# Triangular inverses of the RWKV-7 recurrence kept in a PSUM bank, with the factor stored by rows

## The chip, the cores and the metric

One core of a Trainium2 chip runs the whole kernel. The metric is device microseconds of one execution, as the median of several runs. The engines are named as in the profile: PE (matrix multiplies, with PEld for its weight loads), DVE (vector engine), ACT (scalar engine), POOL, and SP, whose queue issues the DMAs.

## The reference, cut to what matters

The kernel computes two decoder layers on 1024 tokens of width 1024. In each layer a normalised input goes through one input projection; its columns feed three token mixers (an RWKV-7 recurrence with 4 heads of 64, a dilated attention, a latent attention); an output projection and a SwiGLU feed-forward follow. The change lies in the recurrence, which the reference writes as a scan over tokens:

```python
def step(state, inp):
    r_t, w_t, k_t, v_t, kk_t, b_t = inp
    sa = jnp.einsum('bhvk,bhk->bhv', state, kk_t)
    state = (state * w_t[:, :, None, :] - sa[..., None] * b_t[:, :, None, :]
             + v_t[..., None] * k_t[:, :, None, :])
    y = jnp.einsum('bhvk,bhk->bhv', state, r_t)
    return state, y
```

The kernel does this in chunks of 64 tokens. Inside a chunk the terms `sa` depend on each other through a lower triangular 64x64 matrix, so each pair of chunk and head needs the inverse of a unit triangular matrix.

## The kernel before, in words

**Work and its order.** The 1024 tokens are two halves (`hf` 0 and 1) of 512; tiles are 128 partitions x 512 floats (a page in SBUF, a bank in PSUM). All steps are Python generators ("strands"). While the program is built, the class `Flow` plays them against a clock per engine: each helper books a cost (`tt` on DVE 1.04 ns a column and 65 ns, `vtrans` 1.1 ns a column and 65 ns, `acopy` 0.833 ns a column and 80 ns), a result is usable 150 ns (PE 230 ns) later (`LATENCY`, line 106), and the strand that can start first goes next (`run`, line 172), with a lower number as the stronger priority at ties. The order found so is the order of each engine's queue in the program, and an engine never leaves that order on the chip: if an instruction at the head of a queue waits, all behind it wait. The costs are guesses of the plan; the chip's are in the profile.

**Pages and banks.** `page`/`pages` take SBUF pages from a pool of 79, `bank` (line 351) takes one of the 8 PSUM banks, `free` gives them back. `in_proj` (line 1094), the input projection, runs with a weak priority (6) and asks with `bank("inp", 4)` (line 1142): it takes a bank only when at least 4 others stay free. One output tile of it is 24 matmuls; it is emptied by DVE in the first half of layer 0, otherwise by ACT (`evac`, line 1022). Its weights are fetched by `loader` (line 475): a DMA brings `wr`, ACT makes the rounded part `wh` and POOL (sometimes DVE) the rest `wl`; up to 6 such pairs lie ready (`ring`).

**The recurrence.** `recurrence(hf)` (line 1211) has priority 0 and runs four times in all (two layers, two halves). After the Gram matrices `Gm` (32 pairs of chunk and head, each 128 x 128, in `a1`) are there, it inverts the 32 triangular matrices, each as two 32x32 blocks on the diagonal that are then joined:

- Four DVE transposes (line 1425) write `NL`, 128 partitions x 32 x 32: partitions 0 to 63 hold the two diagonal blocks of all 32 pairs, and partitions 64 to 127 the same again. A partition's element is `NL[p, t, s]`, the factor of row t and column s.
- A DMA brings `first`, the rows of unit matrices, into the page `W` (line 1429); the lower and the upper 64 partitions hold the even and the odd rows.
- 31 steps of two DVE instructions each (lines 1432 to 1438). Step s works on n x m columns, n = s // 2 + 1 and m = 31 - s, 2856 columns over the 31 steps: the first instruction multiplies one column of `W` with one column of the factor into `tmp`, the second takes `tmp` from `W`. Each needs the result of the one before.
- Two ACT copies bring the halves of `W` together as `W2` (line 1442), two DVE transposes put the inverses into `TT` (line 1450), and one more makes `T1` in the tile `T1Y` (line 1454).
- `merge` (line 1457) joins the blocks: 32 small matmuls "mg" a half with `T1`, an ACT copy into `T1Y`, 32 more matmuls, an ACT copy into `TT`. Then the chunks follow one after the other.

Beside this run the input projection of the same or the next half and, in the first half, `rates` (line 1226), whose matmuls "lo" need `xw` from DVE.

Of the kernel before, what the change touches and what calls it, by code (L numbers as in the profile page):

```python
# [14 lines left out]
ALU = mybir.AluOpType  # L15
# [207 lines left out]
def cols(ap):  # L223
    n = 1
    for d in ap.shape[1:]:
        n *= d
    return n
# [3 lines left out]
def trunk(ctx: ExitStack, tc: tile.TileContext, xT, pos, vec, con, first, w_in, small, uq, uqr, ukv,  # L231
# [3 lines left out]
    F = Flow()  # L235
# [56 lines left out]
    def acopy(out, in_):  # L292
        F.op("act", cols(in_) * 0.833 + 80)
        nc.scalar.copy(out=out, in_=in_)  # L294
# [3 lines left out]
    def tt(eng, out, a, b, op):  # L298
        F.op(eng, cols(out) * (1.04 if eng == "dve" else 2.2) + 65)
        ENG[eng].tensor_tensor(out=out, in0=a, in1=b, op=op)  # L300
# [18 lines left out]
    def vtrans(out, in_):  # L319
        F.op("dve", cols(in_) * 1.1 + 65)  # L320
        nc.vector.transpose(out=out, in_=in_)

    def dma(out, in_, nbytes):

        s = F.cur
        start = max(s.at(), F.clock["dma"])
        F.clock["dma"] = start + max(450.0, nbytes / 360.0)
        nc.sync.dma_start(out=out, in_=in_)
        return F.clock["dma"] + 2000
# [21 lines left out]
    def bank(name="ps", keep=0, n=None):  # L351
        yield Need([banks], n or 1, keep)
        out = []
        for _ in range(n or 1):
            t = psp.tile([128, HALF], F32, tag="ps", name=name)
            owner[id(t)] = (banks, t, None)
            out.append(t)
        return out if n else out[0]
# [7 lines left out]
    def pages(where, names, dt=F32, keep=0, of=None):  # L366

        def taken(n):
            if of in reserve:
                reserve[of] -= n  # L370

        got = yield Need(lambda: [P[w] for w in where], len(names), keep, taken if of else None)
        of = of if of in reserve else None
        out = []
        for n, s in zip(names, got):
            n, d = n if isinstance(n, tuple) else (n, dt)
            t = s.pool.tile([128, HALF], d, tag="hp", name=n)
            owner[id(t)] = (s, t, of)
            out.append(t)
        return out  # L380

    def page(where, name, dt=F32, keep=0, of=None):
        return (yield from pages(where, [name], dt, keep, of))[0]

    def free(*tiles):
        for t in tiles:
            s, _, of = owner.pop(id(t))
            if of is few:
                F.give(few)
            elif of in reserve:  # L390
                reserve[of] += 1
            F.give(s)
# [213 lines left out]
    W = Lookup()  # L606
# [62 lines left out]
    def head_rsqrt(sq, col, guard, op):  # L669

        s = yield from bank("hsum")
        yield "pe"
        for c in range(4):
            mm(s[:, 2 * c:2 * c + 2], sq[:, c * 128:(c + 1) * 128], cons[:, CON[col]:CON[col] + 2], True, True)
        y = yield from rsqrt(s[:, 0:8], 8, guard, op)
        yield "dve"
        vcopy(sq.rearrange("p (a b) -> p a b", b=64), y.unsqueeze(2).to_broadcast([128, 8, 64]))
        yield "pe"
        for c in range(4):
            cs_ = slice(c * 128, (c + 1) * 128)  # L680
            transpose(s[:, cs_], sq[:, cs_])
        return s
# [33 lines left out]
    def events(*shape):  # L716
        if len(shape) == 1:
            return [Event() for _ in range(shape[0])]
        return [events(*shape[1:]) for _ in range(shape[0])]
# [247 lines left out]
    def layer(l):  # L967
# [243 lines left out]
        def recurrence(hf):  # L1211
# [4 lines left out]
            AP_ = ["gp"]  # L1216
# [83 lines left out]
            for j in range(2):  # L1300
# [4 lines left out]
                p = yield from head_rsqrt(sq, "hones", 1e-24, ALU.max)  # L1305
# [62 lines left out]
                p = yield from bank("bn")  # L1368
# [48 lines left out]


            NL = a1.tile([128, 32, 32], F32, tag="NL", name="NL")
            for hb in range(2):  # L1420
                src = Gm[32 * hb:32 * hb + 32, :, 32 * hb:32 * hb + 32].rearrange("p u t -> p t u")
                for ig in range(2):
                    o = 64 * ig + 32 * hb
                    yield "dve"
                    vtrans(NL[o:o + 32], src)
            w_init = Event()
            W_, tmp = yield from pages(AP_, ["W", "tmp"])
            yield "dma"
            F.set(w_init, None, dma(W_, first, 262144))
            yield w_init  # L1430
            Wt = W_.rearrange("p (i t) -> p i t", t=32)
            for s in range(31):
                n, m = s // 2 + 1, 31 - s
                t3 = tmp[:, 0:n * m].rearrange("p (i t) -> p i t", t=m)
                yield "dve"
                tt("dve", t3, Wt[:, 0:n, s:s + 1].to_broadcast([128, n, m]),
                   NL[:, s + 1:, s].unsqueeze(1).to_broadcast([128, n, m]), ALU.mult)
                tt("dve", Wt[:, 0:n, s + 1:], Wt[:, 0:n, s + 1:], t3, ALU.subtract)
            W2 = a1.tile([128, 16, 2, 32], F32, tag="NL", name="W2")
            for ig in range(2):  # L1440
                yield "act"
                acopy(W2[0:64, :, ig, :], Wt[64 * ig:64 * ig + 64])
            free(W_, tmp)
            yield "pool"
            F.op("pool", 1000)
            nc.gpsimd.memset(TT[32:64, :, 0:32], 0.0)
            for hb in range(2):
                r = slice(32 * hb, 32 * hb + 32)
                yield "dve"
                vtrans(TT[r, :, r].rearrange("p u t -> p t u"), W2[r].rearrange("p i g t -> p t (i g)"))  # L1450
            T1Y = a1.tile([128, 32, 32], F32, tag="NL", name="T1Y")
            T1, Ys = T1Y[0:32], T1Y
# [996 lines left out]
        for hf in range(2):  # L2449
            F.spawn(recurrence(hf), 0)  # L2450
# [179 lines left out]
```

## Time and profile before

| | |
|---|---|
| median of 3 runs | 2693.75 us (2692.81 to 2708.47) |
| the profiled execution | 2702.44 us, of which 2700.4 us lie between its first and last instruction (the span) |
| busy in the span | PE 2569.5 us, DVE 1865.0, POOL 1266.2, ACT 1146.0 |
| the four inverses, from the first transpose to `T1Y` | 126.8 to 177.9, 268.5 to 322.1, 1448.9 to 1491.4, 1615.9 to 1660.5 us |

Times in the rows are microseconds from the start of the span unless marked ns. In a timeline, the bracket behind an instruction gives the time for which its engine was idle before it, and what ended that. The tile `W2` shows under the name W, since it is read from W, and PEclk is the clock granted to PE as a share of the full one. Matmuls overlap, so the time that each shows is longer than the distance to the next.

### The profile page before, as it was taken

The page shows a single profiled execution, that of the slowest core. Times are in us where ns is not written, and L with a number is a line of the kernel's source. Part 1 is how long each engine was busy: PE and PEld are TensorE (multiplying, and loading weights), DVE is VectorE, ACT ScalarE, POOL GpSimd, SP SyncE. Part 2 cuts the span into 40 slices and gives each one's busy share as a digit, 9 for nine tenths or more (in the row PEclk, how much of TensorE's full clock was granted, in tenths as well). Part 3 has the DMA queues.
Part 4 walks back from the last instruction along what each step waited for, and adds up shares of the span by engine and source line. Part 5 has one row for each costly group of instructions (what it writes and reads, how often), then busy time and mean ns, then how long its engine had stood idle before and what let it go on. Part 6 is the DMA issues. An engine that isn't in the chain of part 4 may idle for free. (4 is left out here: it accounts for less than half of the span.)

```text
span 2700.4 us, 38578 instructions
## 1 busy us (share of the span) xinstructions
PE 2569.5 (95%) x13112; PEld 2055.7 (76%) x13112; DVE 1865.0 (69%) x3539; ACT 1146.0 (42%) x2312; POOL 1266.2 (47%) x978
## 2 busy tenths in 40 slices
PE   7989898999999999999999998999998999999998
PEld 6766765788777888888878676657887888888887
DVE  7988758765778676556578477577558876665556
ACT  5344357564434343322343433656644343333221
POOL 4635332346654444465554354223566444444561
PEclk9889899999999999999999898999999999999999
DMA  5222202026435444796332121101363454349861
GB/s 183 80 90 87 75 9 73 21 69 205 148 133 187 152 172 151 259 343 224 131 124 84 60 75 40 52 26 40 102 215 110 164 195 144 137 158 336 285 208 63
DMA packets 204772, 365.08 MB, mean 135 GB/s; under 512 B 23712, under 2 KB 38304, under 8 KB 204448
## 3 DMA queue, kind: packets, MB, share of 16 engines
q1 hardware_dynamic: 204576, 362.63, 39.3%
q8 instruction: 103, 1.69, 0.2%
q14 instruction: 93, 0.76, 0.1%
HBM read 253.22 MB, written 105.64 MB: 133 GB/s over the span
## 5 line engine op out<-in xcount | busy, mean ns | idle before, releaser
L300 POOL TENSOR_TENSOR wl<-wr,wh 128x512 fp32r<-128x512 f32 (+1 forms) x376 | 546.9, 1466 | 515.3 <-ACT wh L294 450.3
L265 PE MATMUL gu<-hhi,wh 128*128 128x512 f32 x1232 | 484.0, 393 | 18.5 <-ACT u L294 12.4
L265 PE MATMUL gu<-hhi,wl 128*128 128x512 f32 x1232 | 480.5, 391 | 1.1 <-POOL wl L300 1.0
L265 PE MATMUL gu<-hlo,wh 128*128 128x512 f32 x1232 | 481.4, 391 | 0.0
L294 ACT CAST wh<-wr 128x512 fp32r<-128x512 f32 (+1 forms) x496 | 287.3, 597 | 127.4 <-POOL wl L300 38.9
L265 PEld LDWEIGHTS gu<-hhi,wh 128*128 128x128 f32 x1232 | 232.5, 189 | 76.8 <-ACT u L294 15.3
L265 PEld LDWEIGHTS gu<-hhi,wl 128*128 128x128 f32 x1232 | 232.4, 189 | 50.9 <-POOL wl L300 2.0
L265 PEld LDWEIGHTS gu<-hlo,wh 128*128 128x128 f32 x1232 | 232.7, 189 | 47.2
L300 POOL TENSOR_TENSOR wl<-s,wh 128x512 fp32r<-128x512 f32 (+1 forms) x136 | 180.0, 1332 | 188.1 <-ACT wh L294 93.6
L265 PE MATMUL dn<-bhi,wh 128*128 128x512 f32 (+1 forms) x664 | 251.7, 380 | 0.7 <-issue 0.7
L265 PE MATMUL dn<-bhi,wl 128*128 128x512 f32 (+1 forms) x664 | 251.5, 379 | 0.0
L265 PE MATMUL dn<-blo,wh 128*128 128x512 f32 (+1 forms) x664 | 251.5, 379 | 0.0
L265 PE MATMUL inp<-hhi,wh 128*128 128x512 f32 x512 | 220.1, 430 | 14.5 <-ACT wh L294 14.5
L294 ACT CAST wh<-s 128x512 fp32r<-128x512 f32 (+1 forms) x204 | 116.6, 581 | 228.4 <-DVE s L300 198.2
L265 PE MATMUL inp<-hlo,wh 128*128 128x512 f32 x512 | 210.3, 411 | 0.0
L265 PE MATMUL inp<-hhi,wl 128*128 128x512 f32 x512 | 209.7, 410 | 0.5 <-POOL wl L300 0.3
L300 DVE TENSOR_TENSOR x<-x,dn 128x512 f32<-128x512 f32 (+1 forms) x160 | 104.5, 657 | 109.3 <-PE dn L265 82.2
L300 DVE TENSOR_TENSOR v<-u,gu 128x512 f32<-128x512 f32 x132 | 90.1, 682 | 128.6 <-PE gu L265 125.1
L300 POOL TENSOR_TENSOR v<-v 128x512 f32<-128x512 f32 x66 | 97.1, 1473 | 136.1 <-DVE v L300 127.0
L265 PEld LDWEIGHTS dn<-bhi,wh 128*128 128x128 f32 x664 | 124.9, 188 | 25.0 <-issue 1.5
L265 PEld LDWEIGHTS dn<-bhi,wl 128*128 128x128 f32 x664 | 124.9, 188 | 23.5
L265 PEld LDWEIGHTS dn<-blo,wh 128*128 128x128 f32 x664 | 124.9, 188 | 23.3
(314 smaller groups left out, 5536.0 us busy)
## 6 DMA issues: line engine op xcount, KB each, us to landing
wr<-in_w_in_dram SPq DMA_DIRECT2D x144, 256.0 KB
act_dram<-ahi SPq DMA_DIRECT2D x142, 256.0 KB
act_dram<-alo SPq DMA_DIRECT2D x142, 256.0 KB
bhi<-act_dram SPq DMA_DIRECT2D x142, 256.0 KB
blo<-act_dram SPq DMA_DIRECT2D x142, 256.0 KB
wr<-in_w_gate_dram SPq DMA_DIRECT2D x104, 256.0 KB
wr<-in_w_up_dram SPq DMA_DIRECT2D x104, 256.0 KB
wr<-in_w_down_dram SPq DMA_DIRECT2D x96, 192.0 KB
```

The costliest lines, as they stand in the source:

```text
L265: nc.tensor.matmul(out=out, lhsT=lhsT, rhs=rhs, start=start, stop=stop, **kw)
L294: nc.scalar.copy(out=out, in_=in_)
L300: ENG[eng].tensor_tensor(out=out, in0=a, in1=b, op=op)
```

## The change

The 64x512 halves stay as they are, but `W` becomes `Wp`, a PSUM bank. The DMA brings `first` into the page `tmp`, and a small strand `init` of priority 0 lets ACT copy it to the bank. Two DVE transposes rather than four write `NL`, only its partitions 0 to 63, and with the two axes exchanged, so that `NL[p, s, t]` has one step's factors side by side; one ACT copy repeats them in partitions 64 to 127. The steps read `NL[:, s, s+1:]`. The bank is given back where the page `W` was.

```diff
             NL = a1.tile([128, 32, 32], F32, tag="NL", name="NL")
+            tmp = yield from page(AP_, "tmp")
+            Wp = yield from bank("Wp")
+            yield "dma"
+            w_init, w_set = events(2)
+            F.set(w_init, None, dma(tmp, first, 262144))
+
+            def init():
+                yield w_init
+                yield "act"
+                acopy(Wp, tmp)
+                F.set(w_set)
+
+            F.spawn(init(), 0)
             for hb in range(2):
                 src = Gm[32 * hb:32 * hb + 32, :, 32 * hb:32 * hb + 32].rearrange("p u t -> p t u")
-                for ig in range(2):
-                    o = 64 * ig + 32 * hb
-                    yield "dve"
-                    vtrans(NL[o:o + 32], src)
-            w_init = Event()
-            W_, tmp = yield from pages(AP_, ["W", "tmp"])
-            yield "dma"
-            F.set(w_init, None, dma(W_, first, 262144))
-            yield w_init
-            Wt = W_.rearrange("p (i t) -> p i t", t=32)
+                o = 32 * hb
+                yield "dve"
+                vtrans(NL[o:o + 32].rearrange("p s t -> p t s"), src)
+            yield "act"
+            acopy(NL[64:128], NL[0:64])
+            yield w_set
+            Wt = Wp.rearrange("p (i t) -> p i t", t=32)
             for s in range(31):
                 n, m = s // 2 + 1, 31 - s
                 t3 = tmp[:, 0:n * m].rearrange("p (i t) -> p i t", t=m)
                 yield "dve"
                 tt("dve", t3, Wt[:, 0:n, s:s + 1].to_broadcast([128, n, m]),
-                   NL[:, s + 1:, s].unsqueeze(1).to_broadcast([128, n, m]), ALU.mult)
+                   NL[:, s, s + 1:].unsqueeze(1).to_broadcast([128, n, m]), ALU.mult)
                 tt("dve", Wt[:, 0:n, s + 1:], Wt[:, 0:n, s + 1:], t3, ALU.subtract)
             W2 = a1.tile([128, 16, 2, 32], F32, tag="NL", name="W2")
             for ig in range(2):
                 yield "act"
                 acopy(W2[0:64, :, ig, :], Wt[64 * ig:64 * ig + 64])
-            free(W_, tmp)
+            free(Wp, tmp)
```

## Rows read from the trace of the kernel before

**Rows 1.** The page, busy tenths of PE and its granted clock in 40 slices.
```profile
PE   7989898999999999999999998999998999999998
...
PEclk9889899999999999999999898999999999999999
```

**Rows 2.** Windows over the four inverses: busy time of each engine.
```profile
126.80:177.90 51.10, 39.18 (x196) 32.74 (x194) 48.86 (x93) 15.25 (x24) 19.19 (x14) 0.91 0.45 144
268.50:322.10 53.60, 44.25 (x230) 38.05 (x230) 49.36 (x111) 15.98 (x29) 20.28 (x17) 0.91 0.25 87
...
sum 191.80, PE 158.44 PEld 135.60 DVE 178.72 ACT 54.75 POOL 75.55; mean PE 39.61 PEld 33.90 DVE 44.68 ACT 13.69 POOL 18.89
```

**Rows 3.** Timeline of PE: its long waits at the end of the inverses.
```profile
176.64 0.79 PE L265 MATMUL lo<-xw,whi 128*128 128x512 f32 x1 [11.92 <-DVE xw L300]
...
322.13 3.62 PE L265 MATMUL mg<-T1Y,Gm 32*32 32x32 f32 x64 [7.68 <-DVE T1Y L321]
...
1491.34 3.62 PE L265 MATMUL mg<-T1Y,Gm 32*32 32x32 f32 x64 [7.21 <-DVE T1Y L321]
...
1653.87 0.80 PE L265 MATMUL inp<-hhi,wh 128*128 128x512 f32 x1 [4.75 <-ACT wh L294]
...
1672.48 3.62 PE L265 MATMUL mg<-TT,T1Y 32*32 32x32 f32 x64 [5.99 <-ACT T1Y L294]
```

**Rows 4.** Windows behind these waits; the third number from the right is PEclk.
```profile
176.60:186.30 9.70, 9.66 (x24) 6.45 (x25) 6.63 (x19) 4.37 (x6) 2.41 (x2) 0.51 0.11 43
322.10:333.60 11.50, 11.47 (x148) 10.38 (x149) 2.54 (x4) 4.56 (x9) 2.57 (x3) 0.50 0.13 36
1491.30:1504.20 12.90, 12.86 (x150) 11.00 (x150) 1.51 (x3) 4.87 (x10) 2.86 (x3) 0.52 0.35 120
1653.80:1657.10 3.30, 3.10 (x7) 2.00 (x8) 2.75 (x3) 3.25 (x8) 3.20 (x3) 0.51 0.09 16
1672.40:1684.60 12.20, 12.12 (x92) 9.57 (x93) 5.79 (x7) 4.27 (x10) 2.17 (x2) 0.50 0.03 6
```

**Rows 5.** Timeline of ACT: what stands behind its copies of W in its queue.
```profile
1484.33 1.25 ACT L294 COPY W<-W 64x512 f32<-64x512 f32 x2 [13.65 <-DVE W L300]
1485.48 0.57 ACT L294 COPY pj<-inp 128x512 f32<-128x512 f32 x1
...
1652.41 0.62 ACT L294 COPY W<-W 64x512 f32<-64x512 f32 x1 [14.10 <-DVE W L300]
...
1653.20 0.62 ACT L294 CAST wh<-wr 128x512 fp32r<-128x512 f32 x1
```

**Rows 6.** Windows of the steps' instructions alone (tile tmp), one inverse and the sum.
```profile
1448.90:1491.40 42.50, 25.00 (x62) 0.94 0.34 110
...
sum 191.80, DVE 98.76; mean DVE 24.69
```

**Rows 7.** Groups of DVE instructions by shape: busy us, mean ns, idle before.
```profile
L300 DVE TENSOR_TENSOR W<-W,tmp 128x30 f32<-128x30 f32 x8 | 1.5, 189 | 0.2
L300 DVE TENSOR_TENSOR W<-W,tmp 128x130 f32<-128x130 f32 x4 | 1.2, 296 | 0.1
L300 DVE TENSOR_TENSOR W<-W,tmp 128x128 f32<-128x128 f32 x4 | 1.2, 293 | 0.1
L300 DVE TENSOR_TENSOR tmp<-W,NL 128x16 f32<-128x16 f32 x4 | 0.7, 180 | 0.1
L300 DVE TENSOR_TENSOR tmp<-W,NL 128x128 f32<-128x128 f32 x4 | 1.6, 400 | 0.1
L300 DVE TENSOR_TENSOR pl<-tp,ph 128x128 fp32r<-128x128 f32 x16 | 4.6, 286 | 2.0 <-ACT ph L294 1.9
L321 DVE STREAM_TRANSPOSE NL<-Gm 32x1024 f32<-32x1024 f32 x16 | 32.2, 2010 | 0.3
L321 DVE STREAM_TRANSPOSE TT<-W 32x1024 f32<-32x1024 f32 x8 | 17.8, 2228 | 3.3 <-ACT W L294 3.2
```

**Rows 8.** Tile Gm on DVE: duration ns min/median/max (operand G in PSUM).
```profile
L300 DVE TENSOR_TENSOR Gm<-G,tabs x32: 672/680/692, 89.6 to 1615.3; 128x512 f32<-128x512 f32 x32
```

**Rows 9.** Timeline of DVE inside the third inverse: two steps' instructions.
```profile
1465.47 1.34 DVE L300 TENSOR_TENSOR tmp<-W,NL 128x110 f32<-128x110 f32 x1
1466.85 0.27 DVE L300 TENSOR_TENSOR W<-W,tmp 128x110 f32<-128x110 f32 x1
```

**Rows 10.** Timeline of POOL at the same time.
```profile
1461.26 5.33 POOL L300 TENSOR_TENSOR wl<-wr,wh 128x512 fp32r<-128x512 f32 x4 [9.49 <-PE vB L265]
```

**Rows 11.** Groups of ACT copies: busy us, mean ns, idle before.
```profile
L294 ACT COPY W<-W 64x512 f32<-64x512 f32 x8 | 4.9, 617 | 41.0 <-DVE W L300 41.0
L294 ACT COPY tabs<-sq 128x1 f32<-128x1 f32 x1 | 0.2, 186 | 0.0
```

**Rows 12.** Window of 15 us in which PE runs the projection at full clock.
```profile
135.00:150.00 15.00, 15.00 (x68) 12.43 (x67) 14.00 (x34) 1.91 (x4) 5.09 (x4) 1.00 0.26 76
```

## The prediction

> **What bounds the kernel now.** I read the page's 40 slices first. PE is busy nine tenths or more in nearly all of them, so a microsecond on another engine counts only where PE waits for it. Among the few slices with an eight for PE are those of the inverses, and the granted clock falls there too [rows 1]. The windows over the four inverses come next: DVE is busy 178.72 of 191.8 us there and PE only 158.44 [rows 2]. So in these stretches DVE is the bound, and PE runs beside it on the input projection until the plan's order brings an instruction that needs the inverse. The timeline of PE shows those points: 11.92, 7.68, 7.21, 4.75 and 5.99 us, 37.6 us in sum [rows 3]. Two wait for `T1Y`, the end of the inverse itself. The first waits for `xw`, which stands on DVE behind the inverse's last transposes. The fourth waits for a weight `wh`, whose cast stands on ACT behind the copy of W, and ACT had then waited 14.10 us for the last step [rows 5]. The fifth waits for ACT's copy into `T1Y`, which stood behind attention casts that waited for DVE. All five are one thing: DVE comes to the end of the 31 steps later than the plan thought.
>
> Each wait has a sequel. Behind it PE runs at 0.50 to 0.52 of its clock, the lower level of 1.2 GHz, for 9.7, 11.5, 12.9, 3.3 and 12.2 us, 49.6 us in all, and is busy all the time [rows 4]. At full clock that work would take about half.
>
> **The transposes of NL.** Four at 2.01 us go [rows 7], 8.04 us. Two come that read as before and write with a stride; the nearest row is TT<-W, strided on both sides, 2.23 us [rows 7], so 4.46 us. The ACT copy of 64x1024 is new: 186 ns for one column and 617 for 512 [rows 11] give 0.84 ns a column and 1.05 us, and I add 0.3 us for the two handovers. The path gets 8.04 - 5.8 = 2.2 us shorter, DVE is relieved of 3.6. Bounds for the two transposes: 2.01 and twice that.
>
> **The steps.** An inverse's 62 instructions take 98.76 / 4 = 24.7 us [rows 6]. The second of a step takes 189 ns at 30 columns and 296 at 130 [rows 7]: 157 ns and 1.07 a column, so over 31 steps and 2856 columns 31 x 0.157 + 2856 x 0.00107 = 7.9 us. The first takes 180 ns at 16 columns and 400 at 128 [rows 7], so 149 ns and 1.96 a column: 10.2 us. It is dearer by column because it reads the factor with a stride of 32 floats, where the second reads rows. What is left, 24.7 - 18.1 = 6.6 us, is neither: a few instructions an inverse take about 1 us more than others of their shape. The product with 110 columns at 1465.47 takes 1.34 us, its neighbour 0.27 [rows 9], while POOL makes four weight parts in a row from 1461.26 to 1466.6 [rows 10]. I counted 9, 6, 7 and 6 such instructions in the four inverses. Both operands of these lie in SBUF. Where one lies in PSUM this does not happen: all 32 products of `Gm` take 672 to 692 ns [rows 8], with POOL as busy.
>
> After the change both instructions have one operand in PSUM, and the first reads rows. If it then costs what the second does, an inverse takes 2 x 7.9 = 15.8 us, 8.9 less (2.3 from the rows, 6.6 from POOL). What a DVE write to PSUM costs, no row shows, since PE alone writes it here. A read costs nothing: 286 ns for pl<-tp,ph with 128 columns from PSUM against 293 for W<-W,tmp from SBUF [rows 7]. Bounds: zero, and a second fixed part of 157 ns on each of the 62, 9.7 us. I take zero, by the nearest row, and keep the other end as a rival.
>
> The Trainium skill speaks against the change here. Its page Perfetto Trace Analysis, section "Optimizing Scalar/DVE Operations", gives a DVE instruction about 60 ns of access overhead on SBUF and about 125 on PSUM. By it, as an estimate, 62 x 65 ns = 4.0 us of an inverse's gain would go; the read rows above disagree with it. By the page's figure up to 4 x 4.0 = 16 us of the waits would stay, and the time would be 2679 us at most.
>
> **The initial copy, bank and page.** ACT's copy of 128x512 into the bank, some 0.6 us [rows 11], lies beside the transposes: the DMA is now issued before them and they take 4.5 us. If the DMA lands late, weight casts wait behind the copy on ACT; the ring of six weight pairs covers that, and without the cover I price it at 2 us an inverse. ACT's 64x1024 copy likewise waits for DVE at the head of ACT's queue, under the same cover. A page less costs nothing. The bank is held some 25 us an inverse; I cost that at nothing, since the projection can keep three tiles instead of four in flight, and the third rival is the case in which that fails.
>
> **The sum.** An inverse ends 2.2 + 8.9 = 11.1 us earlier. The plan sees part of this: two transposes at 1.19 us and 0.15 of latency less, an ACT copy of 0.93 and 0.15 more, 1.6 us net. So PE's instructions that need the inverse move forward by 1.6 us and the result comes 9.5 us closer to them. Of the waits this takes 9.5 of 11.92, all of 7.68, 7.21 and 4.75, and of the last, which depends on other DVE and POOL work too, about half, 3.0: 32.1 us. Of the slow clock, the three stretches whose wait is gone (11.5, 12.9, 3.3 us) give half of their length back, 13.8 us, and the other two (9.7 and 12.2) a quarter, 5.5: 19.3 us. Against this I set what is late next: POOL's weight parts, `xw` behind ACT's table load, the chunk chain. I take one new wait of about 5 us for each inverse, the size of the two shorter ones in rows 3: 20 us. That leaves 32.1 + 19.3 - 20 = 31 us. After the inverses PE is busy to the end [rows 1], so a gain there reaches the end.
>
> The profiled execution took 2702.4 us, so the sum gives 2671; that execution lies 8.7 us above the median of 2693.75, and against the median I predict 2663 us. About 1%, 27 us, is what a measurement of this kernel can tell from no change.
>
> **Rivals.**
> - The order turns against it (half the gain). The plan is made anew: the cheaper transposes and the missing page shift everything behind them, and other late instructions (`xw`, `wh`, the attention's casts) keep PE waiting. For it: three of the five waits are on something other than T1Y itself. Against: all three stand behind the inverse's instructions. Half the waits return, 16 us, and no clock is won; less 3 for reordering: 13 us, 2681.
> - PSUM is dear. With the second fixed part the steps take 15.8 + 9.7 = 25.5 us, what they take now; only the 2.2 us of the transposes are left, less the plan's 1.6, which is nothing at the waits. DVE's relief of 3.6 us an inverse may help by 5 in all: 2689. For it: no row of a DVE write to PSUM. Against: the reads in rows 7 and 8.
> - The bank is missed, and the kernel gets slower. The projection asks for a bank only when four others stay free, so with one held it has three tiles in flight, at 24 matmuls of 15 / 68 us, 5.3 us each [rows 12]. Its tiles are emptied behind the copies of W on ACT (a `pj` at 1485.48 right behind a wait of 13.65 us [rows 5]) or on the full DVE. If that lateness stays over two tiles, 10.6 us, PE stops. Price: one tile's 5.3 us and some 10 us of slow clock behind it, 5 us lost, for each inverse: 41 us, against the half gain of 10 that stays: 2693.75 + 31 = 2725. Against: the lateness itself should fall to about 4 us.
>
> The Trainium skill leans to this rival: the same page, section "Matmul Optimizations", wants all eight PSUM banks used for matmuls. No row here shows fewer banks.
>
> **How the numbers follow.** My forecast has a chance of 0.48, the reordered half gain 0.30, dear PSUM 0.10, the missing bank 0.12. The forecast's own range is 2643 (no new waits, 20 us) to 2675. Faster by over 1% (under 2666.8) is most of the forecast's share and little of the half gain's: 0.46. Slower by over 1% is the bank alone: 0.12. Within 1%: 0.42. The range takes in the half gain and dear PSUM and cuts the bank's upper part: 2638 to 2708.
>
> **What would show it.** In the new profile: 8 transposes into NL near 2.2 us; 62 step instructions of about 15.8 us an inverse with none of 1 us among them, and the first of a step as quick as the second (wrong if the smallest take well over 0.19 us: PSUM is dear); no wait of PE for T1Y, and no stretch at half clock behind it (if they stay while the steps are quicker, it is the order); PE waiting on a bank, with `inp` matmuls released by `pj` or `raw` copies, would be the bank. The prediction is wrong if an inverse shortens by less than 6 us, or if PE's idle time moves elsewhere.

## Result, and the profile after the change

| | before | after |
|---|---|---|
| median | 2699.35 us (4 runs, 2692.81 to 2708.47) | 2667.44 us (4 runs, 2663.63 to 2675.43) |
| ratio, 95% interval | | 0.9872 [0.9849, 0.9895] |
| profiled execution, its span | 2702.44, 2700.4 us | 2675.43, 2673.5 us |
| DVE busy in the span | 1865.0 us | 1822.3 us |

The kernel is 1.28% faster, and the whole interval lies beyond 1%. The prediction of 2663 us is 4.4 us under the median.

The page's slices of the kernel after, answering to [rows 1]:

```profile
PE   7999898999999999999999999999998999999998
...
PEclk9889888999999999999999998999999999999999
```

In the second layer PE's eight in the 25th slice (the fourth inverse) and the clock's in the 23rd and the 25th (the third and the fourth) are gone; the clock's new eight in the 28th slice lies behind the inverses. In the first layer PE's eight in the third slice (the first inverse) is gone, but the clock now shows three eights in a row, slices 5 to 7, some 267 to 468 us, where before it showed one.

The tile of the steps, as in [rows 6], in windows over the four inverses:

```profile
125.10:165.40 40.30, 15.86 (x62) 0.00 (x0) 0.98 0.49 163
260.40:303.10 42.70, 15.85 (x62) 0.58 (x1) 0.93 0.36 118
...
sum 150.80, DVE 63.66 ACT 1.75; mean DVE 15.92 ACT 0.44
```

The 62 instructions take 15.92 us an inverse, where 24.69 were needed before. The number behind each window is its length; the windows follow the inverses, which now last 40.4, 42.6, 31.4 and 36.2 us from the first transpose to `T1Y`. Before they lasted 50.9, 53.5, 42.3 and 44.5: shorter by 10.5, 10.9, 10.9 and 8.3 us.

DVE's groups by shape, answering to [rows 7]:

```profile
L321 DVE STREAM_TRANSPOSE NL<-Gm 32x1024 f32<-32x1024 f32 x8 | 17.8, 2230 | 0.2
L300 DVE TENSOR_TENSOR Wp<-Wp,tmp 128x30 f32<-128x30 f32 x8 | 1.6, 196 | 0.2
L300 DVE TENSOR_TENSOR Wp<-Wp,tmp 128x130 f32<-128x130 f32 x4 | 1.2, 301 | 0.1
L300 DVE TENSOR_TENSOR tmp<-Wp,NL 128x128 f32<-128x128 f32 x4 | 1.2, 291 | 0.1
L300 DVE TENSOR_TENSOR tmp<-Wp,NL 128x16 f32<-128x16 f32 x4 | 0.7, 174 | 0.1
```

The product with 128 columns went from 400 to 291 ns. The subtraction, which now writes PSUM, went from 189 to 196 and from 296 to 301 ns. Its smallest, middle and largest duration stand in the answer for the tile `tmp`:

```profile
L300 DVE TENSOR_TENSOR tmp<-Wp,NL x124: 173/261/300, 131.0 to 1637.7; 128x126 f32<-128x126 f32 x12, 128x30 f32<-128x30 f32 x8, 128x56 f32<-128x56 f32 x8, 128x78 f32<-128x78 f32 x8
L300 DVE TENSOR_TENSOR Wp<-Wp,tmp x124: 181/267/307, 131.2 to 1637.9; 128x126 f32<-128x126 f32 x12, 128x30 f32<-128x30 f32 x8, 128x56 f32<-128x56 f32 x8, 128x78 f32<-128x78 f32 x8
```

None of the 248 takes over 307 ns; the instructions of 1.3 us, such as the one in [rows 9], are gone. ACT's copies, answering to [rows 5] and [rows 11]:

```profile
L294 ACT COPY W<-Wp 64x512 f32<-64x512 f32 x8 | 4.7, 582 | 7.0 <-DVE Wp L300 7.0
L294 ACT COPY NL<-NL 64x1024 f32<-64x1024 f32 x4 | 4.2, 1046 | 13.7 <-DVE NL L321 13.7
L294 ACT COPY Wp<-tmp 128x512 f32<-128x512 f32 x4 | 2.3, 586 | 4.6 <-DVE Gm L300 4.6
```

ACT's idle time ahead of the copies of W fell from 41.0 to 7.0 us. Last, the timeline of PE where [rows 3] showed long waits, with one (at 338.20) that stood behind them:

```profile
164.25 0.80 PE L265 MATMUL lo<-xw,whi 128*128 128x512 f32 x1 [2.73 <-DVE xw L300]
...
303.05 1.16 PE L265 MATMUL mg<-T1Y,Gm 32*32 32x32 f32 x18 [8.17 <-DVE T1Y L321]
...
338.20 1.11 PE L265 MATMUL U<-Xs,TT 64*64 64x64 f32 x8 [2.62 <-DVE Xs L313]
...
1484.27 1.89 PE L265 MATMUL mg<-T1Y,Gm 32*32 32x32 f32 x54
...
1646.75 2.34 PE L265 MATMUL mg<-T1Y,Gm 32*32 32x32 f32 x64 [1.16 <-DVE T1Y L321]
...
1650.90 3.62 PE L265 MATMUL mg<-TT,T1Y 32*32 32x32 f32 x64 [0.33 <-ACT T1Y L294]
```

The waits of 11.92, 7.21, 4.75 and 5.99 us have become 2.73, none, none and 0.33. The one of 7.68 us, at the second inverse, is still there and is 8.17 us, although that inverse ends 19.1 us earlier (303.0 against 322.1). The stretches behind it:

```profile
303.00:315.50 12.50, 12.46 (x158) 11.68 (x158) 2.55 (x4) 3.43 (x7) 3.04 (x2) 0.56 0.07 12
338.20:356.00 17.80, 17.80 (x91) 12.65 (x92) 5.07 (x9) 8.02 (x16) 9.02 (x8) 0.50 0.00 1
```

PE ran at about its lower level (0.56) for 12.5 us behind the wait for `T1Y`, as in [rows 4], and at that level (0.50) for 17.8 us behind the one of 2.62 us at the chunks' matmuls `U`. A wait there is not new, but what follows it is longer. Before, one of 2.34 us stood ahead of `U` a chunk sooner, and the clock behind it came to 0.63 for 4.6 us:

```profile
352.41 0.50 PE L265 MATMUL U<-Xs,TT 64*64 64x64 f32 x5 [2.34 <-DVE Xs L313]
...
352.40:357.00 4.60, 4.59 (x31) 3.39 (x32) 2.62 (x5) 2.83 (x6) 1.05 (x1) 0.63 0.10 18
```

Where did the 27 us between the spans come from? The feed-forward's matmuls `gu` mark the ends of a layer's first part, the one with the inverses. I call the time up to the first `gu` the first layer, and the time from there to the last `gu` the second. Their line in the two kernels, before and then after (the first and the last start are the two numbers behind the durations):

```profile
L265 PE MATMUL gu<-hhi,wh x1232: 387/389/796, 699.5 to 2468.1; 128*128 128x512 f32 x176
```

```profile
L265 PE MATMUL gu<-hhi,wh x1232: 387/389/796, 702.8 to 2440.8; 128*128 128x512 f32 x176
```

The first `gu` starts 3.3 us later than before. From there to the last it takes 1738.0 us, not 1768.6: all of the gain, 30.6 us, is the second layer's. These are single executions. In two runs described below whose second layer is that of before (the idle bank, the first layer alone) it took 1761.1 and 1760.5 us, so the share of the change is 22 to 31 us.

### The profile page after: what moved, and what is told of

Read it like the earlier page. It is cut to its first block, busy times and chain, and to the rows that moved or that the text cites. A ratio compares the mean times of both kernels' runs of the same rounds, so it can differ in the third digit from the quotient of the medians.

```text
span 2673.5 us, 38613 instructions
## 1 busy us (share of the span) xinstructions
PE 2564.4 (96%) x13112; PEld 2053.2 (77%) x13112; DVE 1822.3 (68%) x3535; ACT 1154.0 (43%) x2319; POOL 1269.6 (47%) x978
## 5 line engine op out<-in xcount | busy, mean ns | idle before, releaser
L265 PEld LDWEIGHTS dn<-bhi,wh 128*128 128x128 f32 x664 | 124.9, 188 | 25.2 <-issue 1.5
```

The costliest lines, as they stand in the source:

```text
L265: nc.tensor.matmul(out=out, lhsT=lhsT, rhs=rhs, start=start, stop=stop, **kw)
```

## The experiments

The theory: what counts is when the chain of an inverse ends against the place at which PE's queue asks for it, so a shorter chain pays until it meets that place, and each part of the change pays by the microseconds that it takes off the chain. The rival: the gain is another order of the queues, which any edit of the plan could bring. The bank as a cost stood beside both.

**The bank alone** (`e1_bank_alone`). The kernel after, with the four transposes and the column reads of before:

```diff
-                vtrans(NL[o:o + 32].rearrange("p s t -> p t s"), src)
-            yield "act"
-            acopy(NL[64:128], NL[0:64])
+                for ig in range(2):
+                    o = 64 * ig + 32 * hb
+                    yield "dve"
+                    vtrans(NL[o:o + 32], src)
...
-                   NL[:, s, s + 1:].unsqueeze(1).to_broadcast([128, n, m]), ALU.mult)
+                   NL[:, s + 1:, s].unsqueeze(1).to_broadcast([128, n, m]), ALU.mult)
```

> The matrix W lies in the PSUM bank, but four transposes write NL as in the kernel before and the steps read the factor by columns. Theory (the length of the inverse decides): the instructions slowed by POOL go, the columns stay dear, so the 62 step instructions take about 18.2 us an inverse instead of 24.7 and the path is 6.5 us shorter of the 11 that the whole change saves; of its 34 us about 20 come, ratio near 0.993. Rival (the new order of the queues decides): the matmuls mg stand in PE's queue behind 462, 696, 1164 and 1494 matmuls inp in the four inverses, nearly as in the changed kernel (456, 696, 1161, 1497), so nearly all of the gain comes, ratio near 0.988.

Measured: 2667.05 us (2660.08 to 2671.74), ratio 0.9876 [0.9850, 0.9902], as much as the whole change: the rival's number (0.988), not the theory's (0.993). **The rows alone** (`e2_rows_alone`) is the opposite: the kernel before, W in SBUF, with the lines that the diff above takes out.

> Two transposes, the ACT copy of NL and steps that read rows, but W in an SBUF page, brought by the DMA as before. Theory (length): POOL's slowing of 6.6 us an inverse stays, the products fall from 10.2 to 7.9 us and the transposes' part from 8.0 to 5.8, so the path is 4.5 us shorter: about 14 us of the 34, ratio near 0.995. Rival (order): mg stands behind 462, 696, 1170 and 1497 matmuls inp, nearly as in the changed kernel, so nearly all of the gain comes, ratio near 0.988.

Measured: 2682.57 us (2677.35 to 2690.27), ratio 0.9925 [0.9887, 0.9962]: the theory's 0.995 lies within, the rival's 0.988 just outside. The steps' time in the two kernels, summed over windows that hold all four inverses, the bank alone first:

```profile
sum 580.00, DVE 71.74 ACT 2.37; mean DVE 35.87 ACT 1.18
```

```profile
sum 580.00, DVE 96.03; mean DVE 48.02
```

An inverse's steps take 24.7 us before, 71.74 / 4 = 17.9 with the bank alone, 96.03 / 4 = 24.0 with rows alone and 15.9 with both. So the bank takes 6.8 us off and the rows 2.0 more; without the bank the rows bring 0.7, since more instructions then meet POOL: on DVE's timeline 33 of the steps' 248 take over 0.9 us, 26 before. The timelines of POOL and of DVE with rows alone show how:

```profile
133.09 8.81 POOL L300 TENSOR_TENSOR wl<-wr,wh 128x512 fp32r<-128x512 f32 x7 [8.11 <-ACT wh L294]
```

```profile
134.48 1.22 DVE L300 TENSOR_TENSOR tmp<-W,NL 128x30 f32<-128x30 f32 x1
135.73 1.22 DVE L300 TENSOR_TENSOR W<-W,tmp 128x30 f32<-128x30 f32 x1
136.98 1.25 DVE L300 TENSOR_TENSOR tmp<-W,NL 128x58 f32<-128x58 f32 x1
138.27 1.22 DVE L300 TENSOR_TENSOR W<-W,tmp 128x58 f32<-128x58 f32 x1
```

POOL makes seven weight parts, 8.81 / 7 = 1.26 us each, and each of DVE's instructions takes one such part's time, whether it has 30 or 58 columns.

By chain length the theory fails on size: with the bank alone the inverses last 47.6, 43.4, 35.6 and 37.6 us, on average 6.7 shorter than before, against 10.1 in the whole change, and yet the time is the same. Part of the answer is the place: in that kernel 183 of the first layer's later projection matmuls `vB` stand ahead of the second merge in PE's queue, in the changed kernel 120. PE then waits 5.62 us for the second inverse, not 8.17, and the first `gu` comes at 692.4 us, not 702.8. The other part is that the second layer has no more to give: from the first `gu` to the last it takes 1738.0 us with the bank alone and 1738.0 with the whole change (1747.0 with the rows alone, 1768.6 before). This is the theory's "until it meets that place"; the expectation had priced each microsecond alike.

**Which operand** (`e10_products_in_bank`). Rows alone, with the products `tmp` in a bank and `W` in SBUF:

```diff
-            W_, tmp = yield from pages(AP_, ["W", "tmp"])
+            W_ = yield from page(AP_, "W")
+            tmp = yield from bank("tmp")
```

> As e2_rows_alone, W in SBUF and the factor read by rows, but the products are written to a PSUM bank. So the first instruction of a step reads two operands in SBUF and writes PSUM; the second reads one operand in PSUM and one in SBUF and writes SBUF. If it is two inputs in SBUF that make an instruction wait for POOL, the first kind still shows some of about 1.2 to 1.4 us (maximum over 1 us) and the second none (maximum under 0.35 us); the four inverses' steps then take some 17 to 20 us each. If any operand in PSUM frees an instruction, the output too, neither kind shows one over 0.35 us, and the steps take about 16 us. Ratio 0.983 to 0.997 by either.

Measured: 2678.59 us (2672.43 to 2684.89), ratio 0.9895 [0.9832, 0.9958]. The tile `tmp`:

```profile
L300 DVE TENSOR_TENSOR tmp<-W,NL x124: 185/292/1372, 132.7 to 1641.2; 128x126 f32<-128x126 f32 x12, 128x30 f32<-128x30 f32 x8, 128x56 f32<-128x56 f32 x8, 128x78 f32<-128x78 f32 x8
L300 DVE TENSOR_TENSOR W<-W,tmp x124: 173/259/297, 133.3 to 1641.4; 128x126 f32<-128x126 f32 x12, 128x30 f32<-128x30 f32 x8, 128x56 f32<-128x56 f32 x8, 128x78 f32<-128x78 f32 x8
```

The product, with two inputs in SBUF and its output in PSUM, still goes up to 1372 ns; the subtraction, with one input in PSUM and its output in SBUF, never takes over 297. It is the inputs. The steps came to 87.95 / 4 = 22.0 us, over the 17 to 20 expected, since POOL now meets products more often: 32 of them take over 0.9 us and no subtraction, where with rows alone it was 14 products and 19 subtractions. The Trainium skill's page "SBUF — State Buffer", section "SBUF: two separate sides", says the same: a DVE instruction with two SBUF inputs and a GpSimd one that reads SBUF exclude each other for a whole instruction, and whoever comes second waits.

**A term doubled** (`e3_products_twice`). The kernel after, each product issued twice, the second time unbooked, so that the plan's prices stay:

```diff
                    NL[:, s, s + 1:].unsqueeze(1).to_broadcast([128, n, m]), ALU.mult)
+                nc.vector.tensor_tensor(out=t3, in0=Wt[:, 0:n, s:s + 1].to_broadcast([128, n, m]),
+                                        in1=NL[:, s, s + 1:].unsqueeze(1).to_broadcast([128, n, m]), op=ALU.mult)
```

> The changed kernel with each of the 31 products of an inverse issued twice, the second time with the same result and without a cost in the plan. Theory (length): each inverse gets about 31 products longer, 7.6 us and 0.9 us of gaps, so three quarters of the shortening are given back; PE waits at the four mg again, and some 25 of the 34 us go, ratio near 0.997. Rival (order): mg stands behind 456, 696, 1176 and 1512 matmuls inp, in the first layer exactly as in the changed kernel, so at least the first layer keeps its share, ratio near 0.99.

Measured: 2720.9 us (2718.84 to 2725.14), ratio 1.0075 [1.0051, 1.0100], slower than before. PE's waits in the windows 120 to 345 and 1400 to 1720 us (sum, times, longest):

```profile
PE mg L265 <- DVE T1Y L321: 40.2, 2, 21.2
...
PE mg L265 <- DVE T1Y L321: 25.2, 2, 20.9
```

The steps took 94.93 us in all, 31.3 more than in the changed kernel. The waits for `T1Y` rose from 9.3 to 65.4 us and the time by 0.0203 x 2700 = 55 us. In the first layer PE asks for both inverses behind as many projection matmuls as in the changed kernel, yet it waits 18.95 us (none in the changed kernel) and 21.24 us (8.17), and the first `gu` comes 18.2 us later, at 721.0. So the rival that only the place in PE's queue counts falls here: the theory was right in the direction, though neither named the size. What the run does not give is the price of the products alone, since DVE's order was not held. In the changed kernel 90 instructions other than the steps' run on DVE from the first transpose to `T1Y` in the four inverses; here there are 130, and they take 31.3 us more as well. The inverses thus became 60.6, 55.1, 41.0 and 59.4 us long, 65 us more in sum than in the changed kernel, which is twice what the products cost.

**The bank as a cost** (`e4_idle_bank`). The kernel before, with a bank taken with the pages and given back with them:

```diff
+            held = yield from bank("held")
+            nc.vector.memset(held[:, 0:1], 0.0)
...
-            free(W_, tmp)
+            nc.vector.tensor_copy(out=held[:, 1:2], in_=held[:, 0:1])
+            free(W_, tmp, held)
```

> The kernel before, with one PSUM bank taken while an inverse runs; one column of it is written at the start and read at the end, and nothing else uses it. Theory (length) and rival (order): no change, ratio 0.998 to 1.002; mg stands in PE's queue exactly as before. Rival (the bank is missed): PE runs out of banks beside the steps, 5 to 10 us an inverse, ratio 1.008 to 1.015.

Measured: 2697.48 us (2693.66 to 2710.47), ratio 0.9992 [0.9971, 1.0012]. A bank held through the steps costs nothing that can be seen, and the rival's 1.008 to 1.015 is out. The Trainium skill (page "Perfetto Trace Analysis", section "Matmul Optimizations") wants all eight banks used; in this run it made no difference that one was not.

**One layer each** (`e5_second_layer`, `e6_first_layer`). The new block stands under a condition, the old one in the other branch:

```diff
+            if l == 1:
...
+            else:
```

> The change in the second layer's two inverses only; the first layer is the kernel before. Theory (the trace's reading: the whole gain comes from the second layer, where three waits of PE went, 7.2, 4.75 and most of 5.99 us): ratio 0.987 to 0.990, and the second layer, from the first gu matmul of the first layer to that of the second, is 30 us shorter. Rival (both layers give their half, and the trace of one execution misleads): ratio near 0.994.

> The change in the first layer's two inverses only; the second layer is the kernel before. Theory (in the first layer the gain is given back: mg stands 60 matmuls vB earlier in PE's queue, still waits 8 us for T1Y, and the clock falls behind it): ratio 0.999 to 1.002. Rival (both layers give their half): ratio near 0.994.

Measured: in the second layer alone 2672.49 us (2665.17 to 2695.85), ratio 0.9881 [0.9844, 0.9917]; in the first alone 2706.51 (2695.96 to 2721.73), 0.9998 [0.9966, 1.0030]. The rival's 0.994 lies outside both. The second layer alone took 1735.0 us from first to last `gu`, 33.6 less than before and 25.5 less than with the first layer alone, where 30 were expected. So the gain is the second layer's, and the first gives all of its own back. This also speaks against the place of the merge as the cause there: in the second layer the merges stand 12 and 24 `inp` earlier in PE's queue than before, which by itself would lengthen the waits, and those of 7.21, 4.75 and 5.99 us went.

**The true price in the plan** (`e8_true_price`). `vtrans` books what the transposes cost on the chip:

```diff
-        F.op("dve", cols(in_) * 1.1 + 65)
+        F.op("dve", cols(in_) * 2.1 + 65)
```

> The changed kernel, but the plan books a DVE transpose at 2.1 ns a column, near the 2.2 us that the strided ones take, instead of 1.1. mg stands behind 471 and 1179 inp in the first and third inverse (456 and 1161) and behind 141 vB in the second (120). Theory (arrival): 2.5 us of the 8.2 us wait go and little of the clock, ratio 0.985 to 0.988. Rival (order is luck): no telling, 0.984 to 0.996.

Measured: 2670.72 us (2667.41 to 2675.06), ratio 0.9867 [0.9813, 0.9920], within both ranges, so the run does not tell them apart. A truer plan is not by itself a better one: the wait at the second merge falls to 3.34 us and the time stays.

**The merge later** (`e7_merge_later`, `e11_merge_8_later`). The last transpose of the inverse is booked as if its result came 4 us (8 us) later, so the strands that follow stand further back in the queues; what runs is the same:

```diff
-            vtrans(T1, TT[0:32, :, 0:32])
+            F.op("dve", 1200)
+            F.cur.t += 4000.0
+            nc.vector.transpose(out=T1, in_=TT[0:32, :, 0:32])
```

> The changed kernel, but the plan believes T1Y to be ready 4 us later, so that mg stands later in PE's queue: behind 708 matmuls inp and 192 vB in the second inverse (696 and 120 in the changed kernel, 11 us of PE's work), 12 to 18 inp later in the first and third. Theory (what counts is the end of the inverse against PE's arrival): the wait of 8.2 us in the second inverse goes with the slow clock behind it, 8 to 12 us faster than the changed kernel, ratio near 0.984. Rival (order is luck, another place takes the gain back): ratio 0.988 or above.

> As e7_merge_later, with the merge planned 8 us later rather than 4. The theory expects the wait of 3.45 us that e7_merge_later left in the second inverse to go or fall under 1 us, and no gain elsewhere, since no other wait for T1Y was left there: a ratio of 0.976 to 0.982. The rival (the chunks behind the merge are the bound by now, so a later merge costs what it is later) expects 0.982 to 0.988.

Measured: 2650.16 us (2644.39 to 2662.26), ratio 0.9795 [0.9737, 0.9854], with 4 us, and 2648.98 (2646.96 to 2659.11), 0.9824 [0.9798, 0.9850], with 8. Both are faster than the kernel before. Against the changed kernel, which was timed in another series, the intervals only just meet ([0.9849, 0.9895]), and none of these eight runs is as slow as the changed kernel's fastest (2663.63 us). With 4 us the gain on it, some 17 us by the medians and 21 by the ratios, is more than the 8 to 12 expected. The two intervals overlap, so nothing says which is better. With 8 us the wait of 3.45 us in the second inverse went, as the theory wanted, but the merge's second matmuls now wait 3.37 us for ACT's `T1Y`, and the ratio is the rival's (0.982 to 0.988), while the medians of that series (2648.98 against 2703.8) give 0.980, the theory's. The run does not decide between the two. The line of `gu` with 4 us:

```profile
L265 PE MATMUL gu<-hhi,wh x1232: 387/389/628, 676.2 to 2413.1; 128*128 128x512 f32 x176
```

The second layer takes 2413.1 - 676.2 = 1736.9 us, as in the changed kernel (1738.0). The extra gain lies in the first, which is 26.6 us shorter than in the changed kernel (676.2 against 702.8); with 8 us it is 19.8 us shorter (683.0).

**The place alone** (`e9_before_merge_later`). The same edit, by 4 us, in the kernel before:

> The kernel before, with the slow chain as it is, and only the first merge matmuls planned later (18 projection matmuls, some 4 us, in the first inverse; 36 and 12, some 9.6 us, in the second; 21, some 4.8 us, in the third; 30 earlier in the fourth). The theory (what counts is the end of the chain against the place at which PE asks for it) expects the waits for T1Y, 7.68 and 7.21 us in the kernel before, mostly gone, under 4 us each, while the chain keeps its length of 42 to 54 us and the 11.92 us wait on xw stays; a ratio of 0.990 to 0.997. The rival (the place alone is all, the shorter chain adds nothing) expects what e7_merge_later reached, 0.980 to 0.985. A second rival (a later merge only delays the chunks behind it) expects 1.000 or more.

Measured: 2685.85 us (2676.85 to 2689.05), ratio 0.9935 [0.9909, 0.9961]. Timeline of PE at the first inverse:

```profile
178.08 0.79 PE L265 MATMUL lo<-xw,whi 128*128 128x512 f32 x1 [12.04 <-DVE xw L300]
...
197.09 2.21 PE L265 MATMUL mg<-T1Y,Gm 32*32 32x32 f32 x64
```

The merge's first matmuls wait nowhere longer than 0.22 us for `T1Y`, with a chain as long as before (42.7 to 52.8 us), and the wait for `xw` is as it was. The ratio is the theory's, not the rivals'. But the edit moves more than the first matmuls: all that follows is planned anew (the second inverse starts at 286.0 us, not 268.6), and the merge's second matmuls, which wait for ACT's copy into `T1Y`, now wait three times, at the second inverse thus:

```profile
347.85 1.38 PE L265 MATMUL mg<-TT,T1Y 32*32 32x32 f32 x22 [5.81 <-ACT T1Y L294]
```

The other two wait 2.13 and 6.66 us; before there was one such wait, of 5.99 us [rows 3]. The line of `gu`:

```profile
L265 PE MATMUL gu<-hhi,wh x1232: 387/389/794, 703.8 to 2451.2; 128*128 128x512 f32 x176
```

The second layer takes 1747.4 us, 21.2 less than before; the first ends 4.3 us later. So in the first layer neither the change as it stands (3.3 us later) nor the later place alone (4.3 later) wins anything, and both together win 23.3 us. These are single profiled executions; where the first layer's program was that of before, with the idle bank and with the second layer alone, its `gu` began at 698.3 and 703.7 us, so a few microseconds mean nothing and 23 do. The bank alone, whose second merge happens to stand later, won 7.1 there. In the second layer each alone wins most of what there is (30.6 and 21.2), and both together 31.7; against the other two executions of the second layer of before, each of these is some 8 us less.

## Why the prediction was right, and where it was not

**The chain's parts: right to a tenth or two of a microsecond.** The transposes of NL took 2.23 us each and ACT's copy 1.05, as predicted. The steps took 15.92 us against 15.8. Their two parts, argued from rows of before, were seen singly: 6.6 us for POOL (measured 6.8, by the bank alone) and 2.3 for the rows (2.0, on top of it). A DVE write to PSUM was taken at zero: 5 and 7 ns in the two shapes above, some 0.2 us over 31 subtractions. So dear PSUM falls as a rival, and so does the missing bank. By the Trainium skill's page "Perfetto Trace Analysis", section "Optimizing Scalar/DVE Operations", as an estimate, 65 ns would have come on each of 62; no row shows that.

The inverses became shorter by 10.5, 10.9, 10.9 and 8.3 us, where 11.1 was predicted. The fourth falls short since POOL now holds up others: of the six `pj` instructions of the attention that stand between its steps, with two inputs in SBUF, three took 1.60 to 1.72 us while POOL was busy, and before all took 0.69 or less. One of them before, then after, with POOL's line after:

```profile
1644.49 0.68 DVE L300 TENSOR_TENSOR pj<-pj,ropeC 128x512 f32<-128x512 f32 x1
```

```profile
1629.63 1.72 DVE L300 TENSOR_TENSOR pj<-pj,ropeC 128x512 f32<-128x512 f32 x1
...
1629.51 2.99 POOL L300 TENSOR_TENSOR sw<-sw,ropeS 128x512 f32<-128x512 f32 x2 [4.56 <-DMA sw<-pj]
```

The six took 3.1 us more than before. The prediction took POOL's share off the steps and did not ask what else on the path it could meet.

**Wrong: "PE's instructions that need the inverse move forward by 1.6 us".** That was the net of the plan's booked prices. Counted in the built programs, fewer projection matmuls stand ahead of the merge than before: 12, then 60, 12 and 24. At the distance of those matmuls in the trace (0.227 us for `inp`, 0.12 for `vB`, of which the 60 are), that is 2.7, 7.2, 2.7 and 5.4 us. The text ahead of the prediction says that the plan's order is that of the queues; it is not quite. The changed kernel and the one with the products twice, in which the plan books the same prices, came out with different orders on DVE, so something behind the plan orders again; what it weighs was not looked into.

**So "all of 7.68" was wrong too.** PE asked for the second inverse at 322.13 - 7.68 = 314.45 us before and at 303.05 - 8.17 = 294.88 after: 19.6 us earlier, and the inverse, 19.1 us earlier, met it as late as ever. What became of these 19.6 us can be followed in part. 7.2 are the 60 matmuls, which had to come behind the merge. The next part stands in windows, before and then after:

```profile
340.00:400.00 60.00, 57.51 (x431) 39.59 (x430) 32.47 (x74) 31.13 (x71) 21.18 (x19) 0.97 0.02 5
400.00:460.00 60.00, 52.96 (x252) 33.43 (x250) 51.46 (x171) 42.02 (x99) 19.81 (x15) 0.91 0.27 86
```

```profile
340.00:400.00 60.00, 60.00 (x359) 42.37 (x358) 27.56 (x94) 26.50 (x63) 15.07 (x14) 0.85 0.04 14
400.00:460.00 60.00, 48.76 (x216) 30.86 (x215) 49.82 (x148) 40.18 (x88) 20.73 (x16) 0.86 0.24 73
```

From 340 to 460 us PE was idle for 11.2 us, 1.7 more than before, and lost 15.8 us to the lower clock (busy time by what PEclk lacks to 1), 9.3 more: the wait of 2.62 us at 338.20 with its 17.8 us at half clock is most of it. It is not the chance of one execution: by the same two windows 15.9 us went to the clock with the change in the first layer alone, and 6.5 and 8.2 in the two runs with the first layer of before. That makes 18.2 of the 22.9 us between 19.6 won and 3.3 lost; the rest isn't assigned.

**The ledger was right in sum, not in its parts, and that the number came so near is luck.** Of the 37.6 us in [rows 3], the sum took off 32.1; 2.73 + 8.17 + 1.16 + 0.33 = 12.4 are left, so 25.2 went. The clock was to give back 19.3 us. Summed over windows of 10 us, the loss to it up to 700 us and from 1340 to 2000 us went from 31.5 + 32.7 to 40.5 + 20.4: 3.3 us won in all, 12.3 in the second layer less 9.0 in the first. Other executions of the same stretches lost 25.0 and 37.7 (first layer before), 25.8 and 22.0 (second layer before), 35.2 (first after) and 15.2 (second after), so these differences are uncertain by some 10 us each; that the clock gave back far less than 19.3 stands by the means too, which give 2.6. And "one new wait of about 5 us for each inverse", 20 us in sum, was not what came: no such wait in the second layer, and the whole give-back in the first. Two errors, too much gained and too much given back, met at 31 us against the 27 of the profiled executions. Split by layers, the prediction's own terms give 15 us for the first (9.5 and 7.68 of waits, 2.4 and 5.75 of clock, less 10) and 16 for the second; the runs with one layer changed gave nothing for the first and some 32 us (1.19%) for the second. By its own sign, waits for `T1Y` that stay while the steps are quicker, the first layer went the way of its first rival, the order.

**Not foreseen at all** was that the plan's place for the merge is a lever of its own, worth 18 us in the kernel before (2703.8 to 2685.85). The prediction had the rows for it, the waits for `T1Y` in [rows 3], and looked only at moving the chain.

## What to carry to other kernels

When a chain on one engine is shortened, look up where its consumer stands in the other engine's queue after the change: if the queue asks earlier too, the wait stays; here planning the consumer 4 us later took the ratio from 0.987 to 0.980, in two series whose intervals just meet. A DVE instruction whose two tensors both come from SBUF may wait for a POOL instruction each time (1.22 to 1.25 us here for one that takes 0.2); in this kernel one input in PSUM, not the output, freed it, and the write to PSUM cost 5 to 7 ns. What is freed so can leave POOL to meet the next instruction that has both inputs in SBUF. Split a change by layer or stage early, since a total can hide that one stage won everything and another gave all back.

## What the runs showed of the hardware

- What quicker instructions save, meetings with POOL can take back: with rows alone the steps should have lost 2.0 to 2.3 us an inverse and lost 0.7.
- A second input read with a stride of 128 bytes cost 400 ns at 128 columns, the same read by rows 291.
- A wait of 2.62 us on PE was followed by 17.8 us at half clock, longer than the 12.5 us behind one of 8.17; in the kernel before, one of 2.34 us on such matmuls `U` was followed by 4.6 us at a clock of 0.63. The length of a wait did not tell the price behind it.
